# The first store of a multiply-GELU kernel is issued without waiting for a y load

## The chip, the core and the metric

The kernel runs on one core of one Trainium2 chip. The metric is the device time of one execution in microseconds (us). Before the change the median of three runs is 119.92 us (119.90, 119.92 and 120.03).

## What is computed

Two arrays of 1024 x 4096 float32 values are multiplied element by element, and the tanh form of GELU is applied to the product:

```python
z = x * y
return 0.5 * z * (1 + np.tanh(np.sqrt(2 / np.pi) * (z + 0.044715 * z ** 3)))
```

x, y and the output are 16.78 MB each, so 33.55 MB are read from the memory of the chip and 16.78 MB are written back: 50.33 MB in all.

## The kernel before

**Tiling.** The data is flattened and seen as 128 partitions of 32,768 columns. `PIECES` (line 14) cuts the columns into three: a small one, 0 to 1280 (640 KB in all), and two large ones, 1280 to 17664 (16,384 columns, 8.39 MB) and 17664 to 32768 (15,104 columns, 7552 KB). Within a piece each partition's columns lie together in memory, so a transfer is 128 rows, one for each partition: rows of 5,120, 65,536 and 60,416 bytes. The whole of x fits on the chip in `xs`; y goes through the smaller buffer `ys` (20,440 columns), so a later y load overwrites columns that an earlier one has used. The product and the activation are both written in place into `xs`, and the stores leave from there.

**Queues.** Every DMA but one is issued by SyncE (SP) and lies in its queue, which the profile calls q1. The load of the first large x piece is issued by ScalarE (ACT) and lies in q10. SyncE carries out its instructions in the order in which they are written:

1. load x piece 0 (small), put at the very front of the program by `_hoist`, as is ScalarE's load of x piece 1
2. load y for piece 1 (the first y load, `Y_LOADS[0]`)
3. load x piece 2
4. wait until three multiplies are done (`Y_FREE`, line 85), load y for piece 2 (the second y load)
5. wait until four multiplies are done, load y for piece 0 (the last y load, small)
6. the three stores (lines 110 to 114), in the order piece 1, piece 2, piece 0, each after the activations of its piece; the first store also waits for a y load
7. waits for the first two stores (line 116), the clearing of the semaphores (line 119), the wait for the last store (line 120)

**Compute.** For each y load in turn, VectorE waits for the x piece and the y load (lines 93 and 94) and multiplies in steps (`STEPS`, line 20): four steps of 4096 columns for piece 1, seven of 2048 and one of 768 for piece 2, and one of 1280 for piece 0. ScalarE applies the activation to each step as soon as the step's multiply is done (lines 104 to 107). `sem_mul` counts the multiplies and `sem_act` the activations; `done[b]` is the number of activations after which everything up to column b is finished. Each DMA has a semaphore of its own (`sem_x`, `sem_y`, `sem_o`), which stands at 16 when its data has landed.

**The place of the change.** `sem_y[-2]` is the semaphore of the second y load, of piece 2. The list `STORES` begins with piece 1, so at `i == 0` the store of piece 1 is meant. Its data is complete after the fourth activation.

Of the kernel before, what the change touches and what calls it, by code (L numbers as in the profile page):

```python
# [1 line left out]

# [4 lines left out]


F32 = mybir.dt.float32
GELU = mybir.ActivationFunctionType.Gelu_apprx_tanh  # L10

PIECES = [(0, 1280), (1280, 17664), (17664, 32768)]

Y_LOADS = [(1280, 17664, 4056), (17664, 32768, 0), (0, 1280, 15104)]

Y_FREE = [0, 3, 4]

STEPS = [[4096] * 4, [2048] * 7 + [768], [1280]]  # L20
STORES = [(1280, 17664), (17664, 32768), (0, 1280)]
Y_BUF = 20440


def _hoist(nc, issued):

    here = nc.cur_bb.bb.instructions
    first = nc.main_func.blocks[0].instructions
    for ins in issued:
        del here[next(k for k, i in enumerate(here) if i is ins or i.name == ins.name)]  # L30
    engine = issued[0].engine
    at = next(
        k
        for k, i in enumerate(first)
        if i.engine == engine and type(i).__name__ == "InstDrain"
    )
    first[at:at] = issued


@with_exitstack  # L40
def kernel(
    ctx: ExitStack,
    tc: tile.TileContext,
    x: bass.AP,
    y: bass.AP,
    out: bass.AP,
):
    nc = tc.nc
    P = nc.NUM_PARTITIONS

    def columns(t, a, b):

        flat = t.flatten_outer_dims().rearrange("r c -> (r c)")
        pa, pb = next(q for q in PIECES if q[0] <= a and b <= q[1])
        return flat[P * pa : P * pb].rearrange("(p c) -> p c", p=P)[:, a - pa : b - pa]


    tc.close()
    tc.compile()  # L59

    xs = nc.alloc_sbuf_tensor("xs", [P, PIECES[-1][1]], F32).ap()
    ys = nc.alloc_sbuf_tensor("ys", [P, Y_BUF], F32).ap()
    sem_x = [nc.alloc_semaphore(f"sem_x{i}") for i in range(len(PIECES))]
    sem_y = [nc.alloc_semaphore(f"sem_y{i}") for i in range(len(Y_LOADS))]
    sem_mul = nc.alloc_semaphore("sem_mul")
    sem_act = nc.alloc_semaphore("sem_act")
    sem_o = [nc.alloc_semaphore(f"sem_o{i}") for i in range(len(STORES))]

    def load_x(i, engine=nc.sync):
        a, b = PIECES[i]  # L70
        return engine.dma_start(out=xs[:, a:b], in_=columns(x, a, b)).then_inc(sem_x[i], 16)

    def load_y(i):
        a, b, r = Y_LOADS[i]
        return nc.sync.dma_start(
            out=ys[:, r : r + b - a], in_=columns(y, a, b)
        ).then_inc(sem_y[i], 16)

    _hoist(nc, [load_x(0).ins])
    _hoist(nc, [load_x(1, nc.scalar).ins])  # L80
    load_y(0)
    load_x(2)
    for i in range(1, len(Y_LOADS)):
        if Y_FREE[i]:
            nc.sync.wait_ge(sem_mul, Y_FREE[i])
        load_y(i)

    n = 0
    done = {}
    for i, (a, b, r) in enumerate(Y_LOADS):  # L90
        for j, (xa, xb) in enumerate(PIECES):
            if xa <= a < xb:
                nc.vector.wait_ge(sem_x[j], 16)
        nc.vector.wait_ge(sem_y[i], 16)  # L94
        c = a
        for w in STEPS[i]:
            nc.vector.tensor_mul(  # L97
                out=xs[:, c : c + w],
                in0=xs[:, c : c + w],
                in1=ys[:, r + c - a : r + c - a + w],  # L100
            ).then_inc(sem_mul, 1)
            n += 1
            done[c + w] = n
            nc.scalar.wait_ge(sem_mul, n)
            nc.scalar.activation(  # L105
                out=xs[:, c : c + w], in_=xs[:, c : c + w], func=GELU
            ).then_inc(sem_act, 1)
            c += w

    for i, (a, b) in enumerate(STORES):  # L110
        if i == 0:
            nc.sync.wait_ge(sem_y[-2], 16)
        nc.sync.wait_ge(sem_act, done[b])
        nc.sync.dma_start(out=columns(out, a, b), in_=xs[:, a:b]).then_inc(sem_o[i], 16)
    for i in range(len(STORES) - 1):
        nc.sync.wait_ge(sem_o[i], 16)
    nums = sorted(s.num for s in [*sem_x, *sem_y, *sem_o[:-1], sem_mul, sem_act])
    assert nums == list(range(nums[0], nums[-1] + 1))
    nc.sync.sem_clear(range(nums[0], nums[-1] + 1))
    nc.sync.wait_ge(sem_o[-1], 16).then_inc(sem_o[-1], -16)  # L120


# [1 line left out]
_INS = ['x', 'y']  # L124
_OUTS = [((1024, 4096), 'float32')]


# [23 lines left out]
```

## Time and profile before

| what | us |
|---|---|
| median of three runs | 119.92 |
| span of the profiled execution, first to last instruction | 118.3 |
| median above the span | 1.6 |
| VectorE busy (13 multiplies) | 35.2 |
| ScalarE busy (13 activations and a table load) | 31.0 |
| first store issued | 78.02 |
| second and third store issued | 96.30, 97.46 |

The profile's own time for the execution is the span; the runs are timed apart from it, and their median is 1.6 us longer. Times on the page count from the span's start. The page has the busy time of each engine, the load of the DMA queues, the chain of work that ended last, the groups of instructions, and the time of each DMA from issue to landing. A name such as "SPq L114" is an instruction of SyncE's queue on line 114. A DMA is issued in a fraction of a microsecond, but its data moves for as long as "issue to landing" says, behind whatever lies ahead of it. The trace also holds each packet that a DMA engine moved, one for each row and one for each engine's semaphore; the windows give their sum by stretch of time.

### The profile page before, as it was taken

To read this page: it belongs to the slowest core of one execution; us is meant where nothing else is said; L and a number is where in the kernel's file an instruction comes from. 1 tells how busy PE (TensorE), PEld (TensorE's weight loads), DVE (VectorE), ACT (ScalarE), POOL (GpSimd) and SP (SyncE) were. 2 spreads that over 40 slices of the span, in tenths; PEclk is the share of its full clock that TensorE was granted. 3 is DMA by queue.
4 is the path that set the end of the run, shared out by engine and by line. 5 is a ranking of instruction groups with operands and counts; after the bars stand their busy time and mean duration, and the time that the engine had idled before them with its cause. 6 is when DMAs were issued, how large, how long until landed. Compare 5 with 4: busy or idle time off the path is not lost.

```text
span 118.3 us, 82 instructions
## 1 busy us (share of the span) xinstructions
DVE 35.2 (30%) x13; ACT 31.0 (26%) x14; POOL 0.2 (0%) x4
## 2 busy tenths in 40 slices
DVE  0000000000000069999920000059999940000000
ACT  4000000000000001977974000007998990000000
POOL 0000000000000000000000000000000000000000
DMA  9888899889988897797797797798899889977975
GB/s 493 382 382 382 355 643 421 355 355 532 532 355 355 355 654 327 327 654 327 327 654 327 327 654 327 327 576 355 355 643 421 355 355 429 552 327 327 654 327 222
DMA packets 1296, 50.33 MB, mean 426 GB/s; under 512 B 144, under 2 KB 144, under 8 KB 528
## 3 DMA queue, kind: packets, MB, share of 16 engines
q1 hardware_dynamic: 1152, 41.94, 82.2%
q10 hardware_dynamic: 144, 8.39, 16.5%
HBM read 33.55 MB, written 16.78 MB: 426 GB/s over the span
## 4 chain that ended last, share of the span: by engine, by line
DMA 53%; DVE 24%; ACT 3%; issue 1%; DVEq 0%
DMA ys<-in_y_dram 53%; DVE xs L97 24%; ACT xs L105 3%; DVEq L94 0%
## 5 line engine op out<-in xcount | busy, mean ns | idle before, releaser
L97 DVE TENSOR_TENSOR xs<-xs,ys 128x2048 f32<-128x2048 f32 (+3 forms) x13 | 35.2, 2778 | 60.7 <-DMA ys<-in_y_dram 60.7
L105 ACT ACTIVATE xs<-xs 128x2048 f32<-128x2048 f32 (+3 forms) x13 | 29.7, 2301 | 64.9 <-DVE xs L97 64.9
L105 ACT ACT_TABLE_LOAD x1 | 1.3, 1283 | 1.6 <-PEq L59 1.6
L135 POOL MEMSET const-bfloat16-1.0<- 128x1 bf16 x1 | 0.1, 102 | 0.0
L135 POOL MEMSET const-uint8-127<- 128x1 uint8 x1 | 0.1, 102 | 0.0
L135 POOL MEMSET const-float32-0.0<- 128x1 f32 x1 | 0.1, 99 | 0.2 <-issue 0.2
L135 POOL MEMSET const-float32-1.0<- 128x1 f32 x1 | 0.1, 99 | 0.0
## 6 DMA issues: line engine op xcount, KB each, us to landing
xs<-in_x_dram SPq DMA_DIRECT2D x1, 7552.0 KB, 58.2
ys<-in_y_dram SPq DMA_DIRECT2D x1, 7552.0 KB, 22.5
out_dram<-xs SPq DMA_DIRECT2D x1, 7552.0 KB, 20.4
xs<-in_x_dram SPq DMA_DIRECT2D x1, 640.0 KB, 13.3
ys<-in_y_dram SPq DMA_DIRECT2D x1, 640.0 KB, 19.7
out_dram<-xs SPq DMA_DIRECT2D x1, 640.0 KB, 20.8
xs<-in_x_dram ACTq DMA_DIRECT2D x1, 32.5
ys<-in_y_dram SPq DMA_DIRECT2D x1, 40.7
```

The costliest lines, as they stand in the source:

```text
L97: nc.vector.tensor_mul(out=xs[:, c : c + w], in0=xs[:, c : c + w], in1=ys[:, r + c - a : r + c - a + w],).then_inc(sem_mul, 1)
L105: nc.scalar.activation(out=xs[:, c : c + w], in_=xs[:, c : c + w], func=GELU).then_inc(sem_act, 1)
L135: nc = _bacc.Bacc("TRN2", target_bir_lowering=False, num_devices=1)
```

## The change

The first store loses one of its two waits. It waits for its activations alone, as the other two stores do. It stays in the same place in the program and in the same queue, behind the last y load. Loads, compute steps, buffers and the other waits stay as they are.

```diff
     for i, (a, b) in enumerate(STORES):
-        if i == 0:
-            nc.sync.wait_ge(sem_y[-2], 16)
         nc.sync.wait_ge(sem_act, done[b])
         nc.sync.dma_start(out=columns(out, a, b), in_=xs[:, a:b]).then_inc(sem_o[i], 16)
```

## The prediction

> **What bounds the kernel now.** I read the DMA queues first, then the wait table of SyncE's queue, the times from issue to landing, the chain, and last narrow windows around the place of the edit. The queue table says how full the sixteen DMA engines are:
>
> ```profile
> ## 3 DMA queue, kind: packets, MB, share of 16 engines
> q1 hardware_dynamic: 1152, 41.94, 82.2%
> q10 hardware_dynamic: 144, 8.39, 16.5%
> ```
>
> The two queues fill 82.2 + 16.5 = 98.7% of 118.3 us, that is 116.8 us for each engine. The windows below show that nothing moves in the first 1.00 us and nothing after 117.88. That leaves 117.88 - 1.00 - 116.8 = about 0.1 us of idle time per engine between the first packet and the last. The kernel is bound by moving 50.33 MB from end to end, and no new order of the same transfers can win back more than about 0.1 us on an average engine. (An end figure is rounded, so read it as 0 to 0.2.) VectorE at 30% and ScalarE at 26% matter only where they release a store.
>
> The wait table of SyncE's queue has the wait that goes:
>
> ```profile
> SPq L114 <- ACT xs L105: 18.7, 2, 17.9
> SPq L114 <- DMA ys<-in_y_dram: 14.5, 1, 14.5
> SPq L113 <- ACT xs L105: 3.3, 1, 3.3
> ```
>
> Read it from the bottom. SyncE waits for the first group's activations until 63.5 (the timeline starts that instruction at 63.52), then 14.5 us more at the store for the second y load, until 78.02. The top line is the later two stores. A wait of 14.5 us looks like a prize. Whether it is one depends on what the DMA engines do meanwhile, and they hold the rest of y. The issue table:
>
> ```profile
> ys<-in_y_dram SPq DMA_DIRECT2D x1, 7552.0 KB, 22.5
> out_dram<-xs SPq DMA_DIRECT2D x1, 7552.0 KB, 20.4
> ys<-in_y_dram SPq DMA_DIRECT2D x1, 640.0 KB, 19.7
> out_dram<-xs SPq DMA_DIRECT2D x1, 640.0 KB, 20.8
> out_dram<-xs SPq DMA_DIRECT2D x1, 20.9
> ```
>
> The second y load is issued at 55.54 and lands at 78.0; the last, issued at 59.87, lands at 59.87 + 19.7 = 79.6. So when the first store is issued at 78.02 its queue still has about 1.5 us of y ahead of it. The windows (busy, then share of the DMA engines and GB/s; a packet counts whole where it starts) show how well that cover holds:
>
> ```profile
> 0.00:1.00 1.00, 0.00 (x0) 0.00 (x0) 0.20 (x4) 1.00 0.00 0
> 78.02:78.50 0.48, 0.40 (x1) 0.00 (x0) 0.00 (x0) 1.00 0.94 395
> 78.50:78.67 0.17, 0.17 (x1) 0.00 (x0) 0.00 (x0) 1.00 1.01 422
> 78.67:78.86 0.19, 0.19 (x1) 0.00 (x0) 0.00 (x0) 1.00 0.54 216
> 78.86:79.10 0.24, 0.24 (x1) 0.00 (x0) 0.00 (x0) 1.00 8.46 3614
> 79.10:79.20 0.10, 0.10 (x1) 0.00 (x0) 0.00 (x0) 1.00 4.54 1966
> 117.88:118.28 0.40, 0.00 (x0) 0.00 (x0) 0.00 (x0) 1.00 0.00 0
> ```
>
> Full until 78.67; half empty for the next 0.19 us, because some engines have finished y and have no store yet; then the large store packets start, 13 engines by 79.10 and the last three by 79.20. That dent is all that the wait costs.
>
> **The change part by part.**
>
> *The removed wait.* One wait goes. The wait for the activations moves onto the store itself, so a separate instruction of 17 ns on SyncE goes too; it is hidden by 14.5 us of waiting and priced at 0. SyncE issues the first store (0.348 us of its time) at about 63.53 instead of 78.02. Behind it on SyncE stands only the second store's wait for its activation, which ends at 96.29, so no other issue moves.
>
> *What the earlier issue gains, engine by engine.* From the packet records: on each engine the last y load is eight rows of 5,120 bytes at 0.196 us, and its closing semaphore packet ends between 78.69 and 79.20. The first store packets start between 78.864 and 79.192. Pairing both lists in order gives gaps of 0.18, 0.18, 0.15, 0.13, 0.13, 0.13, 0.06, 0.07 and 0.03 us, and 0.01 or none on the other seven: 1.06 us over sixteen engines, 0.07 us on average. With the store already queued each engine goes straight on. So the gain lies between 0.18 us, the largest gap, and nothing, the gap on the last three engines. What ends the kernel is the latest engine. The three late ones start at 79.105, 79.170 and 79.192 and move all 16 large packets of the stores in 2.418 us (65,536 bytes) and 2.229 us (60,416 bytes), the commonest times of these sizes in the load phase too. One of these ends last, at 117.880, and it had no gap. Engines that were early run a few ns slower per packet (2.42 to 2.46 us) and give their lead back; one ends at 117.876. I take 0.03 us, about the middle between the last engine's 0 and the mean 0.07.
>
> A rule on the store's start, in sentences that the sum does without: the issue at 78.02 and the first store packet at 78.864 are 0.84 us apart here. The Trainium skill, "DMA: Bandwidth & Descriptors", section "Specifications", gives about 0.6 us from issue to first byte on this path. By that figure the store would have been ready at 78.62, ahead of the earliest engine's 78.69, and the change would be worth exactly nothing; by the row it is worth the dent above.
>
> *What the early store may cost.* It lies in the queue from 63.5 while 15 us of y loads are still moving ahead of it. The trace has this situation with other names: the second and last y loads lay behind x from 55.5 and 59.9, and the packets ahead kept 2.23 to 2.24 us throughout. So queueing behind costs 0 by the nearest row. New is only that the early engines start writing up to 0.18 us sooner, beside the last y rows of the late ones. The first store packets took 2.45 to 2.46 us on most early engines against 2.418, so 0.036 us is a price of overlap. At the low end the late engine keeps 2.418 (0, as its three now do right behind y packets); at the high end all eight packets of its first store are slowed so, 8 x 0.036 = 0.29 us. I take 0, because the late engines' own first store packets, the nearest row, show 2.418.
>
> A second rule, again outside the sum. The first x load (640 KB on SyncE's queue) took 13.3 us to land, beside a large load on ScalarE's queue, while the second large x load, behind another on SyncE's queue, started only when that had ended. The Trainium skill, same page, section "Queues, rings and completion order", says that an engine alternates packet by packet between the queues it has work for and consumes one queue's descriptors in order. By the first half, a store in another queue would take about half of each engine's time from y; by the second, this store, in the same queue, takes none.
>
> *The compute behind it.* VectorE starts the second group on the second y load's landing at 78.00, and those packets end by 77.65, a microsecond before any store packet could start now. The last y load lands at 79.6 and is first used by the last multiply, at 94.39: cover of 14.8 us. Then the chain:
>
> ```profile
> 78.10 1.52 DVE xs L97
> 80.31 13.31 DVE xs L97 x6
> 93.64 3.80 ACT xs L105 x3
> ```
>
> It gives the second store's issue at 96.30; plus the measured 0.84 its packets are ready at 97.14, and the earliest engine ends the first store at 98.27. That cover of 1.1 us shrinks by the earliest engine's 0.18 to 0.95; gone, each further us of delay would cost a us. The third store, issued at 97.46, is needed at 116.1. Both stay hidden.
>
> *The sum.* 118.3 - 0.03 + 0 = 118.27 us of span. The median of 119.92 lies 1.6 us above the span (start and end of the program, which the edit leaves alone), so 119.89 us. With the bounds: 119.92 - 0.18 = 119.74 to 119.92 + 0.29 = 120.21.
>
> **The rivals.**
>
> *Slower, by mixed traffic.* The late engines keep their 2.418 us only because the others paused. Closed gaps put all sixteen in step, and every store packet of the latest engine costs what the first ones cost now: 16 x 0.036 = 0.58 us, 120.50 us. For it: thirteen engines do run slower than 2.418 during the stores. Against: the mean excess of their later packets is 4 to 10 ns, and the share is 98.7% either way. It decides from 15 ns per packet, 0.24 / 16.
>
> *Slower, by order.* The store does not stay behind y but alternates with it. At 64.4 (63.53 plus the measured 0.84) some 5.8 packets of the second y load remain per engine, as its eight of 2.23 us started near 59.5; each would wait for a store packet of 2.42 us, so it would land 14.0 us later, the chain of 18.3 us would release the second store near 110, and after the first store the engines would idle some 12 us: about 132 us. Against: within SyncE's queue the loads follow one another strictly. It decides from a landing delayed by 0.95 us.
>
> *Faster than can be told from no change.* The unprofiled runs would need a dent that all engines share, of over 0.24 us. The largest gap is 0.18 and the mean idle 0.1; a dent of 0.35 on the latest engine would give 119.57. For it: the spread of the landings (0.5 us) is larger than the gap, and may differ from run to run. Against: the runs lie within 0.13 us of each other.
>
> *That the edit does nothing at all* is no case of its own: the issue moves for certain, and its effect on time is in the forecast.
>
> **How the numbers follow.** About 0.2% (0.24 us) is what a measurement can tell from no change. Forecast, within it, 119.89 us: 0.72. Mixed traffic: 0.13. Order: 0.03. A shared dent: 0.12. Faster 0.12, same 0.72, slower 0.13 + 0.03 = 0.16. The range takes the bounds 119.74 to 120.21 and a part of the two near rivals on either side: 119.68 to 120.30, with about 0.08 left out below and 0.11 above.
>
> **What would show it.** Right: the 14.5 us wait for y is gone; the first store is issued near 63.5 and lands near 98.9, so about 35 us from issue to landing; the window 78.67 to 78.86 holds large store packets on about eight engines; y still lands at 78.0 and 79.6; the second store is still issued near 96.3; the queues still sum to about 98.7%. Wrong: y landing later than 78.5, a first store landing after 99.2, store packets well over 2.43 us on the last engine, or an empty stretch near 98.

## The result and the profile after

The changed kernel takes 120.98 us (median of four runs, 120.87 to 121.11) against 119.91 us before: 1.07 us slower, a ratio of 1.0090 with a 95% interval of 1.0078 to 1.0102. The forecast was 119.89 us, and the result lies above its range.

The profiled execution of the changed kernel took 120.98 us, with a span of 119.7. The DMA queues of its page:

```profile
q1 hardware_dynamic: 1152, 41.94, 82.3%
q10 hardware_dynamic: 144, 8.39, 16.3%
```

The same bytes, and the engines are as busy as before: 98.6% of a longer span. A slower kernel with the same busy share means that the engines worked more slowly somewhere, not that they stood still. The wait table of SyncE's queue, then the line of the timeline with the stores, which gives the first one's issue, then the times from issue to landing. (Line 114 is now the wait for the finished stores, which stood on line 116 before.)

```profile
SPq L112 <- ACT xs L105: 37.0, 3, 32.9
SPq L114 <- DMA out_dram<-xs: 19.5, 1, 19.5
```

```profile
63.82 34.75 SPq L112 DMA_DIRECT2D out_dram<-xs  x3
```

```profile
ys<-in_y_dram SPq DMA_DIRECT2D x1, 7552.0 KB, 22.9
out_dram<-xs SPq DMA_DIRECT2D x1, 7552.0 KB, 21.0
...
ys<-in_y_dram SPq DMA_DIRECT2D x1, 640.0 KB, 20.7
out_dram<-xs SPq DMA_DIRECT2D x1, 640.0 KB, 21.4
```

The wait for y is gone, and the store is issued at 63.82. But the two y loads ahead of it take longer: 22.9 us against 22.5 and 20.7 against 19.7. The small last y load is issued at a fixed point of the compute, so its time to landing is the best measure of what the store does to the loads, and it is used for all experiments below but one. It is 1.0 us longer. From its landing to the landing of the last store the two traces take 38.7 us each, so nothing is lost or won back later: the loss is on y.

Windows around the last y load, first before, then after. The columns are the window, its length, busy time of VectorE, ScalarE and GpSimd, the granted clock, the DMA engines' share and GB/s:

```profile
77.12:78.67 1.55, 0.57 (x1) 0.00 (x0) 0.00 (x0) 1.00 0.93 387
```

```profile
77.61:80.04 2.43, 1.16 (x1) 0.00 (x0) 0.00 (x0) 1.00 0.86 242
80.04:80.60 0.56, 0.56 (x1) 0.00 (x0) 0.00 (x0) 1.00 4.62 1991
```

The windows before and the first of after reach from the first packet of the small load to the moment at which the first engine is done with it; in the second of after the store's packets start. A packet counts whole where it starts. By that count the engines moved 387 GB/s before and 242 after, at a similar busy share (0.93 and 0.86). The rows took longer. The packet records give the amounts: the 128 rows of 5,120 bytes took 0.281 us on average instead of 0.197, which is 0.68 us more over an engine's eight rows, and the last large y row of each engine took 2.68 us instead of 2.23, 0.45 us more. Together that is 1.13 us per engine. All 128 packets of the first store, after them, took 2.418 us. So the early store slowed the rows *ahead* of it, before any packet of its own appears in the record.

### The profile page after: what moved, and what is told of

Its sections match the earlier page's. It is cut to its first block, busy times and chain, and to the rows that moved or that the text cites. A ratio compares the mean times of both kernels' runs of the same rounds, so it can differ in the third digit from the quotient of the medians.

```text
span 119.7 us, 81 instructions
## 1 busy us (share of the span) xinstructions
DVE 35.2 (29%) x13; ACT 31.0 (26%) x14; POOL 0.2 (0%) x4
## 4 chain that ended last, share of the span: by engine, by line
DMA 53%; DVE 24%; ACT 3%; issue 0%; DVEq 0%
DMA ys<-in_y_dram 53%; DVE xs L97 24%; ACT xs L105 3%; DVEq L94 0%
## 6 DMA issues: line engine op xcount, KB each, us to landing
ys<-in_y_dram SPq DMA_DIRECT2D x1, 7552.0 KB, 22.9
ys<-in_y_dram SPq DMA_DIRECT2D x1, 640.0 KB, 20.7
xs<-in_x_dram ACTq DMA_DIRECT2D x1, 32.8
```

## The experiments

**Theory: reads run ahead.** A DMA engine reads ahead of what it is writing. Once the store lies in its queue, it starts to read store rows from the chip's own memory (SBUF) while its last y rows are still on their way from HBM, and these arrive later for it. The store's own rows take 2.418 us each all the same, so what it read early gives nothing back. **Rivals:** large rows behind small ones do harm whatever they are; writing to HBM beside reading does it; the store's reads and the y rows' writes collide in SBUF.

### What kind of transfer has to lie behind y

Three runs put another transfer in the store's place, at the same moment, in the same queue, in each case by one branch in the loop over `STORES`:

```diff
         nc.sync.wait_ge(sem_act, done[b])
+        if i == 0:   # e1: HBM to SBUF
+            nc.sync.dma_start(out=xs[:, a:b], in_=columns(x, a, b)).then_inc(sem_o[i], 16)
+            continue
+        if i == 0:   # e2: HBM to HBM
+            nc.sync.dma_start(out=columns(out, a, b), in_=columns(x, a, b)).then_inc(sem_o[i], 16)
+            continue
+        if i == 0:   # e3: SBUF to SBUF, m = (a + b) // 2
+            nc.sync.dma_start(out=xs[:, m:b], in_=xs[:, a:m]).then_inc(sem_o[i], 16)
+            continue
```

> In place of the first store, at the same moment and in the same place in the queue, the first large x piece is loaded a second time, with the same rows of 65,536 bytes (that piece of the output is not written). The measure is the time of the small last y load from issue to landing: 19.7 us before the change, 20.7 us after it. Theory 'reads run ahead': an engine begins on the store's rows, which lie on the chip, while the last y rows are still on their way, and these lose time to it; a load behind comes from the same far memory and costs nothing: 19.7. Rival 'large rows behind small ones': whatever lies behind the 5,120-byte rows in the queue slows them: 20.7. Rival 'writes': the harm comes from writing to the far memory beside reading: 19.7.

> In place of the first store a copy of the same size from x to the output, both in the chip's memory (HBM), with the same 65,536-byte rows (that piece of the output holds x alone). It writes to HBM as the store does but reads from HBM as the loads do. Theory 'reads run ahead' (the source on the chip matters): small last y load lands after 19.7 to 19.9 us. Rival 'large rows behind small ones': 20.7. Rival 'writes': 20.7.

> In place of the first store a copy within the chip's own memory (SBUF), half of the finished piece over its other half, rows of 32,768 bytes (that piece of the output is not written, and 4.2 MB less are written to HBM). It reads what the store reads and writes nothing to HBM. Theory 'reads run ahead': the small last y load lands after 20.7 us as with the store. Rival 'large rows behind small ones': 20.7. Rival 'writes': 19.7.

The issue tables of the three, in this order:

```profile
ys<-in_y_dram SPq DMA_DIRECT2D x1, 7552.0 KB, 22.5
...
ys<-in_y_dram SPq DMA_DIRECT2D x1, 640.0 KB, 19.7
```

```profile
ys<-in_y_dram SPq DMA_DIRECT2D x1, 7552.0 KB, 22.5
...
ys<-in_y_dram SPq DMA_DIRECT2D x1, 640.0 KB, 19.7
```

```profile
ys<-in_y_dram SPq DMA_DIRECT2D x1, 7552.0 KB, 22.6
...
ys<-in_y_dram SPq DMA_DIRECT2D x1, 640.0 KB, 20.7
```

A load behind y costs y nothing, and neither does a copy within HBM, which writes to HBM as the store does. A copy within SBUF costs the same 1.0 us as the store, though it writes nothing to HBM. By the packet records an engine's last large and eight small y rows lost 0.00, 0.00 and 1.14 us in the three runs. Each was timed once, at 119.84, 125.22 and 118.96 us, against 119.82 for the kernel before; the last moves 4.2 MB less. The two rivals fall: large rows lay behind the small ones in all three, and the one that wrote to HBM without reading SBUF did no harm. What counts is that the transfer behind **reads from SBUF**. (The copy within HBM took longer by itself, 25.3 us from its first packet to its last where the first store took 19.6 before; that accounts for the 125.22 us, lies behind y and is another matter.)

### Whether the small rows are needed

```diff
-Y_LOADS = [(1280, 17664, 4056), (17664, 32768, 0), (0, 1280, 15104)]
+Y_LOADS = [(1280, 17664, 4056), (0, 1280, 0), (17664, 32768, 1280)]
-Y_FREE = [0, 3, 4]
+Y_FREE = [0, 0, 3]
-STEPS = [[4096] * 4, [2048] * 7 + [768], [1280]]
+STEPS = [[4112] * 3 + [4048], [1280], [2048] * 7 + [768]]
-STORES = [(1280, 17664), (17664, 32768), (0, 1280)]
+STORES = [(1280, 17664), (0, 1280), (17664, 32768)]
```

> The changed kernel with the two later y loads in the other order: the small one (5,120-byte rows) goes ahead of the large one, so the store lies behind 60,416-byte rows. Steps of piece 1 are 3 x 4112 and 4048 columns so that the large load still starts after three multiplies; the small piece is stored second. Rival 'large rows behind small ones': without small rows at that place the loss of 1.0 us is gone and the kernel takes 119.8 to 120.0 us, or less. Theory 'reads run ahead', with a fixed amount that is fetched early: the last large rows are slowed instead, and about 1 us stays lost: 120.9 us. 'Writes' expects the loss as well: 120.9 us.

It took 121.22 us, a ratio of 1.0108 (1.0088 to 1.0128) to the kernel before on the same chip. The loss stays. Windows that hold the starts of each engine's second to last y row, and of its last:

```profile
74.54:75.15 0.61, 0.00 (x0) 0.00 (x0) 0.00 (x0) 1.00 3.65 1585
76.76:77.37 0.61, 0.00 (x0) 0.00 (x0) 0.00 (x0) 1.00 5.57 1585
```

A packet counts whole where it starts, so at the same bytes the share gives the ratio of the packet times: 5.57 / 3.65 = 1.53. By the records the last row took 3.40 us instead of 2.23. All of the loss, 1.17 us, now falls on one row of 60,416 bytes, where before it was spread over a large row and eight small ones. Its size is nearly the same, 1.13 and 1.17 us: about the same amount, at whatever rows stand there. (The run is 1.40 us above the kernel before. No run has this order of loads with the wait kept, so the 0.2 us beyond the row's loss stays open.)

### How long the store has to lie there

Idle-time activations on ScalarE after the fourth one of the first group hold the store back; their results go into columns of `ys` that nobody reads any more:

```diff
+            if n == 4:
+                nc.scalar.wait_ge(sem_act, 4)
+                for k, t in enumerate(TIMER):   # [4056] * 3, then also 2100
+                    if k:
+                        nc.scalar.wait_ge(sem_t, k)
+                    nc.scalar.activation(
+                        out=ys[:, 16384 : 16384 + t], in_=xs[:, 1280 : 1280 + t], func=GELU
+                    ).then_inc(sem_t, 1)
...
     for i, (a, b) in enumerate(STORES):
+        if i == 0:
+            nc.sync.wait_ge(sem_t, len(TIMER))
         nc.sync.wait_ge(sem_act, done[b])
```

> The changed kernel, with the first store held by three idle-time activations on ScalarE (results into a part of the y buffer that nobody reads any more), so that it is issued near 74.7 us instead of 63.8, and its rows can be fetched from about 75.5. Theory 'reads run ahead': what counts is that the store lies in the queue before the last 60 to 100 KB of y per engine have gone, not how long; the whole loss stays, and the small last y load lands 20.6 to 20.8 us after its issue. A rival that the store costs for as long as it lies queued would give about a third of the loss or less: 19.9 to 20.1.

> As the run before it, with a fourth activation of 2,100 columns: the first store is issued near 76.7 us and its rows can be fetched from about 77.5, when some 40 KB of y per engine are left (1.5 us). Theory 'reads run ahead': a part of the loss, with y's small rows slowed and its last large row not: 20.0 to 20.5 us to landing for the small last y load, and the large y load lands at 22.5 us as before the change. The rival 'as long as it lies queued' gives 19.8 or less.

Issued at 74.66, the store cost as much as at 63.82 (the y rows of an engine lost 1.14 us); issued at 76.67, hardly anything. For each run the line of the timeline with the stores, then that of the issue table:

```profile
74.66 23.45 SPq L124 DMA_DIRECT2D out_dram<-xs  x3
```

```profile
ys<-in_y_dram SPq DMA_DIRECT2D x1, 640.0 KB, 20.8
```

```profile
76.67 21.43 SPq L124 DMA_DIRECT2D out_dram<-xs  x3
```

```profile
ys<-in_y_dram SPq DMA_DIRECT2D x1, 640.0 KB, 19.8
```

The rival that it costs for as long as it lies queued is out, and it is the first run that rules it out. The second alone would not: its 19.8 us is what that rival said, and my own number was too high (20.0 to 20.5 expected). When the store could be fetched there (76.67 plus the 0.84 us seen before, 77.51), an engine had some 1.5 to 2.0 us of y rows ahead: most of its eight small rows (1.57 us together) and up to 0.4 us of a large one. Its y rows lost 0.17 us, and the run took 120.08 us against 119.89. In the first run, by the same reckoning (75.50), some 3.3 to 4.0 us of y were ahead. So the store does its full harm only if it reaches the engine earlier than in the second run, and 2 us of issue time, from 74.66 to 76.67, lie between all and nearly nothing. The kernel before issues at 78.02, on the safe side.

### How much has to lie there

The first store is cut in two: its first columns go early, the rest keeps the wait for the second y load.

```diff
-STORES = [(1280, 17664), (17664, 32768), (0, 1280)]
+STORES = [(1280, 1280 + THIN), (1280 + THIN, 17664), (17664, 32768), (0, 1280)]
...
-        if i == 0:
+        if i == 1:
             nc.sync.wait_ge(sem_y[-2], 16)
-        nc.sync.wait_ge(sem_act, done[b])
+        nc.sync.wait_ge(sem_act, done[17664 if i == 0 else b])
```

> The kernel before, with the first 256 columns of the first store split off and issued early, behind the y loads (eight rows of 1,024 bytes, 8 KB, on each engine); the rest keeps its wait for the second y load. Theory 'reads run ahead by a fixed amount of about 30 KB': only these 8 KB can be fetched early, and at 27.1 KB per us they cost y 0.30 us: the small last y load lands 20.0 us after its issue. A rival in which any store behind the loads costs the same (a change of direction in the queue): 20.7 us.

> As the run before it with 512 columns, 16 KB on each engine. Theory 'reads run ahead by a fixed amount': 16.4 / 27.1 = 0.60 us, the small last y load lands 20.3 us after its issue. Rival 'change of direction': 20.7 us, the same as with 256 columns.

> The same edit with 1,024 columns: 32 KB on each engine, in eight rows of 4,096 bytes. With 8 KB the small last y load landed 19.7 us after its issue (no loss), with 16 KB 19.8, with the whole store 20.7. Theory 'reads run ahead', amended: some 13 KB fit in without harm and each further KB costs 1/27.1 us up to the full loss: (32.8 - 13.3) / 27.1 = 0.7 us, 20.3 to 20.5 us to landing. Rival 'long rows': short rows cost little whatever their sum, only rows of 32 KB and more do harm: 19.8 us.

> The same edit with 2,048 columns: 64 KB on each engine, in eight rows of 8,192 bytes. Theory 'reads run ahead', amended: more than the engine fetches ahead lies in the queue, so the full loss: 20.6 to 20.8 us to landing, and about 121.0 us in all. Rival 'long rows': 19.8 us to landing.

The lines of the issue tables of the four runs stand first. The table has the early amount on each engine, the landing of the small y load by the issue tables, the mean excess of an engine's last large and eight small y rows by the packet records, and the one time of each run (the kernel before beside them: 119.89 for the first two, 119.77 for the next two):

```profile
ys<-in_y_dram SPq DMA_DIRECT2D x1, 640.0 KB, 19.7
```

```profile
ys<-in_y_dram SPq DMA_DIRECT2D x1, 640.0 KB, 19.8
```

```profile
ys<-in_y_dram SPq DMA_DIRECT2D x1, 640.0 KB, 20.8
```

```profile
ys<-in_y_dram SPq DMA_DIRECT2D x1, 640.0 KB, 21.0
```

| early store | KB per engine | y landing, us | excess of y rows, us | time, us |
|---|---|---|---|---|
| none (before) | 0 | 19.7 | 0.01 | 119.91 |
| 256 columns | 8.2 | 19.7 | 0.00 | 119.96 |
| 512 columns | 16.4 | 19.8 | 0.27 | 120.20 |
| 1,024 columns | 32.8 | 20.8 | 0.93 | 120.93 |
| 2,048 columns | 65.5 | 21.0 | 1.28 | 121.19 |
| all (changed kernel) | 524 | 20.7 | 1.13 | 120.98 |

My first reading, 1/27.1 us for each KB from the first one on, was wrong at both small sizes (0.30 and 0.60 expected). Amended with some 13 KB free, it was too low at 1,024 columns (0.7 expected, and 20.3 to 20.5 us to landing) and a little low at 2,048 (20.6 to 20.8). The excess between 16.4 and 32.8 KB rises by 0.66 us, where 16.4 / 27.1 gives 0.60; carried back, it begins at 16.4 - 0.27 x 27.1 = some 9 KB, and it ends at 1.1 to 1.3 us. This is an estimate from four sizes, each run once; why 2,048 columns cost slightly more than the whole store stays open. The rival "long rows" falls: rows of 4,096 bytes did most of the harm and rows of 8,192 all of it.

### Where the y rows and the store's reads meet

In these runs y rows are written into SBUF while the store reads it. Two runs turn the small last load into a copy of the same rows from HBM to the output in HBM; the first is the kernel before with that, the second the run with the store held by three activations (issued at 74.66 there, at 74.67 here).

```diff
+        if i == len(Y_LOADS) - 1:
+            return nc.sync.dma_start(
+                out=columns(out, a, b), in_=columns(y, a, b)
+            ).then_inc(sem_y[i], 16)
```

> The kernel before (the store waits), with the small last y load turned into a copy of the same rows of y from HBM to the output in HBM, so that these rows aren't written to the chip's own memory (the small piece is multiplied by old contents of the buffer). It is the control for the next run. Both theories expect about the same time for the copy as for the load, 19.7 us from issue to landing, or somewhat more, if a copy within HBM is slower by itself.

> The same copy in place of the small last y load, with the store issued near 74.7 us, as in the run that held it by three idle-time activations; there the loss fell almost whole on the small rows (1.0 of 1.1 us). Theory 'reads run ahead' (the store's reads delay other reads of the same engine, wherever those write to): 1.0 us more than the control from issue to landing. Rival 'the chip's own memory is the place': the store's reads there collide with the y rows' writes there; the copy writes none, so at most 0.2 us more than the control.

The issue tables of the control and of the early store:

```profile
out_dram<-in_y_dram SPq DMA_DIRECT2D x1, 640.0 KB, 19.7
```

```profile
out_dram<-in_y_dram SPq DMA_DIRECT2D x1, 640.0 KB, 21.2
```

The copy, one row of 40,960 bytes on each engine, took 1.51 us in the control and 2.57 us beside the early store: 1.06 us more, without a byte of it being written to SBUF. The last large y row, which is written to SBUF, lost another 0.35 us, so the copy landed 1.5 us later, more than the 1.0 us expected; the times, one run each, are 119.85 and 121.39 us. The rival "SBUF is the place" falls for these rows. The copy within SBUF says the same from another side: a window over most of its rows,

```profile
81.20:88.47 7.27, 7.27 (x4) 6.39 (x4) 0.00 (x0) 1.00 1.00 433
```

shows 433 GB/s, all read from and written to SBUF at once, 27 KB per us on each engine, the rate of a store's rows (65,536 bytes in 2.418 us). Reading and writing SBUF together cost the engines nothing there.

### A version with both advantages

> The kernel with 256 early columns once more, timed in rounds: it closes the gap of up to 0.18 us between y and the first store with work that fetches too little ahead to harm y. Theory 'reads run ahead, the first 13 KB free': 119.8 to 119.95 us, at most 0.1 us below the kernel before, because eight rows of 1,024 bytes take 0.37 us where 8 KB of a long row take 0.30. A rival that any early store costs: 120.2 us or more.

The 256 early columns close the gap between y and the first store and leave y alone (19.7 us to landing), yet it took 119.83 us against 119.77, a ratio of 1.0011 (1.0000 to 1.0022). The eight short rows took 0.37 us where 8 KB of a long row take 0.30, so they cost about the 0.07 us that the gap is worth on an average engine. No version here that computes the whole output beats the kernel before.

## Why the prediction was wrong

**The step that failed** is "queueing behind costs 0 by the nearest row". The row was a load behind a load, and that still holds: the first experiment put a load there, and it cost nothing. A store is another case, because its source is SBUF. Its price is 1.13 us on the y rows of an engine and 1.0 us on the landing of the last one, which is the measured 1.07 us but for 0.07. The remark beside it, that a store in the same queue takes none of y's time because the queue is taken in order, failed in the same way: the order held, and the price did not.

**The unknown cost was bounded at the wrong place.** I looked for the harm in the store's own packets (0.036 us each, up to 0.29 us) and took 0 from the late engines' rows. In the changed kernel the store's packets all took 2.418 us, better than before. The harm fell on the y rows ahead of them. The trace of before held no y row with a store queued behind it early enough, so no row of it could give that price, and the bound had to be wider.

**The gain was right in kind and drowned.** The dent of up to 0.18 us is closed: the first store packets start the moment an engine's last y packet ends (80.05 to 80.59). It is worth at most what was said, and no run here shows that gain by itself.

**"The queues still sum to about 98.7%" came true, and misled.** They sum to 98.6%. I read the share as proof that only 0.1 us could be won, which is right for gains. It says nothing against losses, since a packet that is held up counts as busy.

**The rivals.** Mixed traffic said slower (120.50 us), but by slow store packets, and these did not appear; that the kernel did become slower doesn't speak for it. Order: the store stayed strictly behind y in its queue, and yet harmed what was ahead. The shared dent did not show.

**The compute behind** held as computed. The second y load landed at 78.78, VectorE's second group began at 78.88, and the second store was issued at 97.08, while the earliest engine ended the first store at 99.37. That cover was enough, so the 0.8 us by which y came late did not add a stall of its own.

**The signs named** were right: y landing later than 78.5 (78.78) and a first store landing after 99.2 (100.27) were to show the forecast wrong, and did. Of the lateness at 78.78 some 0.3 us belong to this one execution: the first y load, long before any store, landed at 42.6 instead of 42.3, as it did in the run with 256 early columns, which took 119.96 us.

**What is shown and what is inferred.** Shown: the loss needs a transfer behind y that reads SBUF; it doesn't need writes to HBM, nor y rows that are written to SBUF; it has nearly the same size, 1.13 to 1.28 us behind loads, wherever 66 KB or more per engine lay there early enough (0.93 with 33 KB; 1.41 where the last y rows were copied within HBM instead of loaded). That the engine *reads ahead* into a store of its own is the reading that fits all of it, but no record here shows the reads themselves. The Trainium skill, "DMA: Bandwidth & Descriptors", section "Two DMAs through the same engine are not ordered", says that the descriptors of one queue are pipelined and that an engine's read and write sides are separate queues; a read side ahead of the write side is what these runs need. Why HBM reads behind y do no harm (they may simply arrive after y's) was not tried apart, and no run put the early store into another queue, so whether the shared queue matters is open.

## What to carry to other kernels

Where a queue goes from loads to stores, don't let the store reach the engines while more than some 2 us of loads are still ahead of it (0.17 us was lost with 1.5 to 2.0 us ahead, all of it with 3.3 to 4.0); a wait on the load before the last one, with the last one as cover, is a good way to time it. A wait that the critical chain doesn't name can be worth a microsecond, by what it keeps out of a queue. When a change puts a new kind of transfer behind another, look for a row with the same source and destination; if there is none, the price is unknown on the rows ahead too, and the busy share of the DMA engines can't bound it.

## What the runs showed of the hardware

A transfer that waits its turn in a strict queue slowed the rows ahead of it by 1.1 to 1.4 us per DMA engine when it read from SBUF (store or copy within SBUF, 66 KB or more per engine, early enough), and by 0.00 us when it read from HBM (load or copy within HBM). 8.2 KB per engine of such a store were free. In a copy from HBM to HBM the first row of 65,536 bytes on each engine took 2.42 us, as in a load or store, and the later ones 2.5 to 4.0 (behind the last of them a store lay in the queue); rows of 32,768 bytes within SBUF took 1.213 us, the same rate as a store's.
